# A two-layer pool and attention backbone: where the steps of the modulation chain are drawn

## The chip, the cores and the metric

The kernel runs on one core of one Trainium2 chip. The metric is device time in microseconds (us) of one execution, given as the median of several runs. One further execution was taken with the hardware profiler; all rows below are from it, and their times count from the start of its span.

## The reference, cut to what matters

Layer 0 is a pooling mixer, layer 1 a latent attention; both get their shift, scale and gate from a modulation: SiLU of a conditioning vector times a 2048 x 6144 matrix per layer.

```
for i in range(DEPTH):                       # 2 layers: pool, attention
    shift, scale, gate = split(silu(c) @ ada_w[i] + ada_b[i], 3)      # the same with c_ctx for the context
    h_lat = rms_norm(x, pre_norm[i]) * (1 + scale) + shift            # 512 latent tokens
    h_ctx = rms_norm(ctx, pre_norm[i]) * (1 + scale_c) + shift_c      # 256 context tokens
    ...
    x = x + gate * rms_norm(y_lat, post_norm[i])

def pool_branch(h, w_in, w_grp, b_grp, scale, w_out):                 # width 2048, 4 groups
    u, gate = split(h @ w_in, 2)
    p = centred_multiscale_pool(u)
    p = einsum('blgc,gcd->blgd', p, w_grp) + b_grp
    return (p * scale * silu(gate)) @ w_out
```

Only the pooling layer and the modulation bear on this change; the attention layer runs after it, untouched.

## The kernel before, in words

**Matrix products.** Every product is made of three passes (`mm3`, L198 to L200): each operand is split in a high and a low part, and high x high, high x low and low x high are summed in one PSUM bank. Weights come in pieces of 128 x 1024 values (`wpiece`, L178): a DMA on SyncE's queue (SP) fills one of two `raw` buffers (L186), ScalarE casts it to `whi` (L188), VectorE subtracts to `wlo` (L189); there are four `whi`/`wlo` pairs, and a `raw` buffer is free again when its `wlo` is made.

**The pooling layer** runs in this order. Eight pairs of columns (`gemm1`, j = 0 to 7) give u; eight more, the gate pairs (j = 8 to 15), give the gate: two 128-column blocks over 16 k-tiles, four weight pieces each, and `after(k4)` is called behind each piece. After a gate pair ScalarE copies a column (`gb`, L628) and makes SiLU (`sg`, L631) out of the two halves' banks, with a cast for a later weight piece queued between the halves, VectorE multiplies by the pooled part (L633), and a DMA stores `z1d`. Then `products` (L670) multiplies z by `pool_w_out` in four groups of 512 columns (cc = 0 to 3), eight pieces each; `ahead(n)` is called ahead of each piece of group n. The first group starts in banks that the last gate pair used. `load_z` (L432) brings z back from `z1d`, 128 rows at a time, on the SP queue, and ScalarE (L439) and VectorE (L440) split it into `aL` and `cbig`: four of these tiles are loaded during the last gate pair (into `s2` buffers), twelve during the first group (into three `xt` buffers).

**The modulation chain** (`chain`, `ada_part`, L446) has 128 steps. A step loads 128 x 1024 values of `ada_w` on the SP queue into one of two `araw` buffers (L454) and VectorE adds them, times one SiLU value per row, to two accumulators (L461 twice). After 16 steps TensorE transposes the accumulators (`sums`, L145, 16 transposes in four fours) and VectorE reduces them (L146); the next 16 steps need the accumulators back. `fill(n)` (L519) adds n to a due count and draws that many steps at its place in the program. Before, it is called with 1.4 behind each piece of pairs 1 to 7, 2.2 behind each piece of pairs 8 to 15, 0.4 ahead of each piece of group 0 and 0.9 ahead of those of groups 1 to 3.

**What sets the order.** Each engine and each queue runs its instructions in the order they were put on it. That order is made by a scheduler from the program: it follows the program's order, but takes an instruction early where it reckons the engine free. So a step drawn at one place can stand some way ahead of it on VectorE and on SP.

Of the kernel before, what the change touches and what calls it, by code (L numbers as in the profile page):

```python
# [80 lines left out]
def hybrid_kernel(  # L81
# [176 lines left out]
    def cxs(p, m):  # L258

        at = (4 + m) * 512  # L260
        return banks[:, at:at + CTX + 2]
# [170 lines left out]
    def load_z(z_of, k2):  # L432

        for kt in (2 * k2, 2 * k2 + 1):
            zr = z_of()[:, 0:KEYS]
            nc.sync.dma_start(out=zr, in_=z1d[kt])
            s = pools[:, kt:kt + 1]
            for dst, lo, n in ((aL[kt], 0, SEQ), (aC[:, kt], SEQ, CTX)):
                nc.scalar.activation(dst[:, 0, :], zr[:, lo:lo + n], AF.Copy, scale=s)  # L439
                nc.vector.scalar_tensor_tensor(dst[:, 1, :], zr[:, lo:lo + n], s, f32(dst[:, 0, :]),  # L440
                                               ALU.mult, ALU.subtract)
# [66 lines left out]
    with pool("pa") as ap:  # L508
# [16 lines left out]
        def fill(n):  # L525
            nonlocal due, taken
            due += n
            while due > 0.5:
                due -= 1
                taken += 1  # L530
                next(ada_steps, None)
# [5 lines left out]
        def u_in(ps):  # L537
            for m, u in enumerate(ub):
                nc.scalar.copy(u[:, 3 * PAD + SEQ:3 * PAD + KEYS], cxt(ps, m))
                nc.scalar.copy(u[:, PAD:PAD + SEQ], lat(ps, m))  # L540

        def u_out(g, m, pieces):


            u = ub[m]
            w = WINDOWS[g]
            h = w // 2
            s, step, n = u, 1, ULEN
            while step < w:
                n -= step  # L550
                s2 = ap.tile([P, ULEN], F32, name="s2", tag="s2", bufs=2)
                nc.vector.tensor_add(s2[:, :n], s[:, :n], s[:, step:step + n])
                s, step = s2, 2 * step
            b0 = PAD - h
            at = 0
            for lo, n in ((b0, h), (b0 + SEQ - h + 1, 2 * PAD + w - 1), (b0 + SPAN - h + 1, h - 1)):
                if n:
                    nc.vector.tensor_mul(s[:, lo:lo + n], s[:, lo:lo + n], edget[:, g, at:at + n])
                at += n
            nc.vector.scalar_tensor_tensor(s[:, b0:b0 + SPAN], s[:, b0:b0 + SPAN], 1.0 / w, u[:, PAD:PAD + SPAN],  # L560
                                           ALU.mult, ALU.subtract)
            hi = ap.tile([P, SPAN], F32R, name="ph", tag="ph", bufs=4)
            lo = ap.tile([P, SPAN], F32R, name="pl", tag="pl", bufs=4)
            nc.scalar.copy(hi, s[:, b0:b0 + SPAN])
            nc.vector.tensor_sub(lo, s[:, b0:b0 + SPAN], f32(hi))
            pieces.append((hi, lo))

        def gemm1(col, ways, after):

            ps = pair()  # L570
            for k4 in range(4):
                piece = wblock(w_in[k4 * 4 * P:(k4 + 1) * 4 * P, col:col + 2 * P], 4, 2 * P)
                todo = [(m, way, k) for k in range(4) for m in range(2) for way in ways]
                if k4 == 0:
                    todo.sort(key=lambda t: t[1] is ways[1])
                for m, (fn, a_), k in todo:
                    kt = 4 * k4 + k
                    mm3(fn(ps, m), wt(piece, k, m * P, P), a_(kt), kt == 0, kt == KT - 1)
                after(k4)
            return ps  # L580

        def group(g, pieces):

            for pr_ in range(2):
                wg = wblock(pool_w_grp[0, g, :, pr_ * 2 * P:(pr_ + 1) * 2 * P], 4, 2 * P)
                ps = pair()
                for fn, lo, n in ((lat, 0, SEQ), (cxt, SEQ + 2 * PAD, CTX)):
                    for m in range(2):
                        for k in range(4):
                            hi, low = pieces[k]  # L590
                            mm3(fn(ps, m), wt(wg, k, m * P, P), (hi[:, lo:lo + n], low[:, lo:lo + n]), k == 0, k == 3)
                for m in range(2):
                    dt = g * 4 + pr_ * 2 + m
                    yo = ap.tile([P, KEYS], F32, name="sg", tag="sg", bufs=3)
                    for fn, lo, n in ((cxt, SEQ, CTX), (lat, 0, SEQ)):
                        nc.scalar.activation(yo[:, lo:lo + n], fn(ps, m), AF.Identity, bias=poolb[:, dt:dt + 1])
                    nc.gpsimd.dma_start(out=y1d[dt], in_=yo)
# [3 lines left out]
        NP = 2 * GROUPS  # L601
        pieces = [[] for _ in range(GROUPS)]
        u_in(first)
        for j in range(1, 2 * NP):
            if j == NP:
                assert taken >= 32
            if j == 2 * NP - 1:
                assert taken >= 96
            def after(k4):
                if j <= NP and k4 < 2:  # L610
                    u_out((j - 1) // 2, k4, pieces[(j - 1) // 2])
                fill(1.4 if j < NP else 2.2)
                if j == 2 * NP - 1 and k4 in (1, 2):
                    load_z(lambda: ap.tile([P, ULEN], F32, name="s2", tag="s2", bufs=2), k4 - 1)

            ps = gemm1(j * 2 * P, WAYS if j < NP else GATES, after)
            if j < NP:
                u_in(ps)
            else:
                gated = []  # L620
                for m in range(2):
                    yin = ap.tile([P, ULEN], F32, name="s2", tag="s2", bufs=2)[:, 0:KEYS]
                    nc.gpsimd.dma_start(out=yin, in_=y1d[2 * (j - NP) + m])
                    sg = ap.tile([P, KEYS], F32, name="sg", tag="sg", bufs=3)
                    gated.append((sg, yin))
                gb = small.tile([P, 2, 2], F32, name="gb")
                for m in range(2):
                    nc.scalar.copy(gb[:, m], cxs(ps, m)[:, CTX:])  # L628
                for v, fn, lo, n in ((1, cxs, SEQ, CTX), (0, lat, 0, SEQ)):
                    for m in range(2):  # L630
                        nc.scalar.activation(gated[m][0][:, lo:lo + n], fn(ps, m)[:, 0:n], AF.Silu, bias=gb[:, m, v:v + 1])  # L631
                for m, (sg, yin) in enumerate(gated):
                    nc.vector.tensor_mul(sg, sg, yin)  # L633
                    nc.gpsimd.dma_start(out=z1d[2 * (j - NP) + m], in_=sg)
            if j % 2 == 0 and j <= NP:
                group(j // 2 - 1, pieces[j // 2 - 1])
# [26 lines left out]
    with pool("pb") as bp:  # L663
# [68 lines left out]

        def ahead(n):
            def step(k2):
                fill(0.4 if n == 0 else 0.9)
                if n in (0, 3):
                    (x_ahead if n else z_ahead)(k2)
            return step
# [465 lines left out]
```

## Time and profile before

| | |
|---|---|
| median of 3 runs | 1925.75 us (1922.88 to 1927.26) |
| profiled execution: its own time, its span | 1930.69 us, 1928.8 us |
| TensorE matmuls | 1875.1 us busy, 97% of the span |
| VectorE | 1190.4 us, 62% |
| ScalarE | 652.3 us, 34% |
| DMA, mean over the span | 155 GB/s |
| chain that ended last | TensorE 79%, DMA 10%, VectorE 6% |

TensorE is the engine to look at: it is busy nearly all the time, so a microsecond counts only where TensorE waits, or where its granted clock is low. Its busy time is a model (matmuls are pipelined), so distances between starts of matmuls are the surer measure. The rows read from the trace stand in a section of their own.

### The profile page before, as it was taken

To read this page: it belongs to the slowest core of one execution; us is meant where nothing else is said; L and a number is where in the kernel's file an instruction comes from. 1 tells how busy PE (TensorE), PEld (TensorE's weight loads), DVE (VectorE), ACT (ScalarE), POOL (GpSimd) and SP (SyncE) were. 2 spreads that over 40 slices of the span, in tenths; PEclk is the share of its full clock that TensorE was granted. 3 is DMA by queue.
4 is the path that set the end of the run, shared out by engine and by line. 5 is a ranking of instruction groups with operands and counts; after the bars stand their busy time and mean duration, and the time that the engine had idled before them with its cause. 6 is when DMAs were issued, how large, how long until landed. Compare 5 with 4: busy or idle time off the path is not lost.

```text
span 1928.8 us, 26041 instructions
## 1 busy us (share of the span) xinstructions
PE 1875.1 (97%) x10458; PEld 1618.6 (84%) x10458; DVE 1190.4 (62%) x1516; ACT 652.3 (34%) x1024; POOL 110.7 (6%) x201
## 2 busy tenths in 40 slices
PE   5999999999999979999999999999999999999998
PEld 3788888888888867887888988778999999998886
DVE  5778395877588878634764255635566667665333
ACT  6632222212111124223743232124434444444230
POOL 1000000000000000001010002200000000000000
PEclk9999999999999999999999999999999999999999
DMA  8746273557577777644751237843111112116334
GB/s 301 246 147 197 85 229 99 186 169 232 172 251 228 238 268 229 194 147 162 269 171 44 76 88 254 291 142 93 56 40 54 56 50 67 50 60 191 104 125 153
DMA packets 168105, 299.74 MB, mean 155 GB/s; under 512 B 19592, under 2 KB 89504, under 8 KB 166704
## 3 DMA queue, kind: packets, MB, share of 16 engines
q1 hardware_dynamic: 152800, 243.84, 39.6%
q0 software_dynamic: 13872, 52.07, 7.9%
q10 hardware_dynamic: 1312, 2.16, 0.3%
q8 instruction: 82, 1.34, 0.3%
q14 instruction: 39, 0.32, 0.1%
HBM read 268.65 MB, written 29.38 MB: 155 GB/s over the span
## 4 chain that ended last, share of the span: by engine, by line
PE 79%; DMA 10%; DVE 6%; issue 2%; ACT 2%; POOL 1%; SPq 0%; DVEq 0%; POOLq 0%; ACTq 0%
PE banks L198 24%; PE banks L199 24%; PE banks L200 24%; DMA garaw<-in_ada_w 3%; DMA araw<-in_ada_w 2%; PE banks L1087 2%; DVE acc L461 2%; DMA raw<-in_ada_w 1%; DVE wlo L189 1%; PE banks L1066 1%; PE banks L1067 1%; DMA xt<-z1d 1%; PE banks L145 1%; DMA xs<-in_x 1%; PE banks L227 1%
## 5 line engine op out<-in xcount | busy, mean ns | idle before, releaser
L189 DVE TENSOR_TENSOR wlo<-raw,whi 128x1024 fp32r<-128x1024 f32 (+1 forms) x276 | 328.8, 1195 | 316.0 <-ACT whi L188 314.5
L188 ACT CAST whi<-raw 128x1024 fp32r<-128x1024 f32 (+1 forms) x276 | 283.5, 1029 | 675.4 <-PE banks L200 245.9
L461 DVE SCALAR_TENSOR_TENSOR acc<-araw,sc,acc 128x1024 f32<-128x1024 f32 x240 | 297.6, 1280 | 45.1 <-DMA araw<-in_ada_w 44.7
L198 PE MATMUL banks<-aL,whi 128*128 128x512 f32 x768 | 303.8, 396 | 4.0 <-ACT sg L817 2.0
L200 PE MATMUL banks<-aL,wlo 128*128 128x512 f32 x768 | 302.4, 394 | 2.9 <-DVE wlo L189 2.9
L199 PE MATMUL banks<-aL,whi 128*128 128x512 f32 x768 | 303.3, 395 | 0.0
L199 PE MATMUL banks<-cbig,whi 128*128 128x256 f32 (+2 forms) x640 | 188.4, 294 | 0.0
L198 PE MATMUL banks<-cbig,whi 128*128 128x256 f32 (+2 forms) x640 | 187.8, 294 | 0.4 <-ACT cbig L290 0.4
L200 PE MATMUL banks<-cbig,wlo 128*128 128x256 f32 (+2 forms) x640 | 187.3, 293 | 0.0
L198 PE MATMUL banks<-whi,aL 128*128 128x512 f32 (+1 forms) x448 | 164.8, 368 | 10.4 <-ACT gb L628 6.9
L200 PEld LDWEIGHTS banks<-aL,wlo 128*128 128x128 f32 x768 | 144.7, 188 | 34.9 <-DVE wlo L189 4.2
L199 PE MATMUL banks<-wlo,aL 128*128 128x512 f32 (+1 forms) x448 | 164.2, 367 | 0.0
L200 PE MATMUL banks<-whi,aL 128*128 128x512 f32 (+1 forms) x448 | 164.0, 367 | 0.1
L198 PEld LDWEIGHTS banks<-aL,whi 128*128 128x128 f32 x768 | 145.0, 189 | 20.4 <-ACT aL L290 3.7
L199 PEld LDWEIGHTS banks<-aL,whi 128*128 128x128 f32 x768 | 145.4, 189 | 14.6
L198 PEld LDWEIGHTS banks<-cbig,whi 128*128 128x128 f32 x640 | 120.3, 188 | 21.6 <-ACT cbig L290 1.3
L199 PEld LDWEIGHTS banks<-cbig,whi 128*128 128x128 f32 x640 | 120.5, 188 | 19.7
L199 PE MATMUL banks<-wlo,cbig 128*128 128x256 f32 (+2 forms) x384 | 123.8, 322 | 1.9 <-DVE wlo L189 1.8
L198 PE MATMUL banks<-whi,cbig 128*128 128x256 f32 (+2 forms) x384 | 124.8, 325 | 0.1
L200 PEld LDWEIGHTS banks<-cbig,wlo 128*128 128x128 f32 x640 | 121.3, 189 | 3.4
L200 PE MATMUL banks<-whi,cbig 128*128 128x256 f32 (+2 forms) x384 | 123.5, 322 | 0.0
L198 PEld LDWEIGHTS banks<-whi,aL 128*128 128x128 f32 x448 | 84.8, 189 | 23.9 <-ACT gb L628 7.2
(234 smaller groups left out, 3294.3 us busy)
## 6 DMA issues: line engine op xcount, KB each, us to landing
araw<-in_ada_w SPq DMA_DIRECT2D x128, 512.0 KB, 4.3
raw<-in_pool_w_in SPq DMA_DIRECT2D x64, 512.0 KB, 4.8
raw<-in_pool_w_out SPq DMA_DIRECT2D x60, 512.0 KB, 4.7
raw<-in_mla_w_in SPq DMA_DIRECT2D x40, 512.0 KB, 4.0
raw<-in_ada_w SPq DMA_DIRECT2D x32, 512.0 KB, 4.8
garaw<-in_ada_w POOLq DMA_DIRECT2D x32, 512.0 KB, 5.5
raw<-in_mla_w_out SPq DMA_DIRECT2D x32, 512.0 KB, 3.9
raw<-in_mla_w_ukv SPq DMA_DIRECT2D x32, 256.0 KB, 3.3
```

What stands on the lines that cost most here:

```text
L145: nc.tensor.transpose(pt[:, k * P:(k + 1) * P], acc[:, (lo + k) * P:(lo + k + 1) * P], ident)
L188: nc.scalar.copy(hi[:, :n], raw[:, :n])
L189: nc.vector.tensor_sub(lo[:, :n], raw[:, :n], f32(hi[:, :n]))
L198: nc.tensor.matmul(o, l[0], r[0], start=start, stop=False)
L199: nc.tensor.matmul(o, l[0], r[1], start=False, stop=False)
L200: nc.tensor.matmul(o, l[1], r[0], start=False, stop=stop)
L227: nc.tensor.transpose(pt[:, t * P:(t + 1) * P], xt[:, kt * P:(kt + 1) * P], ident)
L461: nc.vector.scalar_tensor_tensor(acc[v], raw, w, acc[v], ALU.mult, ALU.add)
L1066: nc.tensor.matmul(to, qr[:, o], krh[:, ks], start=True, stop=False)
L1067: nc.tensor.matmul(to, qr[:, o], krl[:, ks], start=False, stop=False)
L1087: nc.tensor.transpose(pt[:, t * P:(t + 1) * P], pr[:, t * P:(t + 1) * P], ident)
```

## The change

`fill` is no longer called in the last gate pair (j = 15), nor ahead of the first four pieces of output group 0. Instead the other pairs draw a tenth more per piece (1.5 and 2.3), and from the fifth piece of group 0 on every piece draws 0.85.

```
             def after(k4):
                 if j <= NP and k4 < 2:
                     u_out((j - 1) // 2, k4, pieces[(j - 1) // 2])
-                fill(1.4 if j < NP else 2.2)
+                if j < 2 * NP - 1:
+                    fill(1.5 if j < NP else 2.3)
                 if j == 2 * NP - 1 and k4 in (1, 2):
                     load_z(lambda: ap.tile([P, ULEN], F32, name="s2", tag="s2", bufs=2), k4 - 1)
...
         def ahead(n):
             def step(k2):
-                fill(0.4 if n == 0 else 0.9)
+                fill(0.85 if n or k2 >= 4 else 0)
                 if n in (0, 3):
                     (x_ahead if n else z_ahead)(k2)
             return step
```

In the program's order the count drawn at the end of pair 14, of pair 15 and of group 0 was 101, 110 and 113; it is now 106, 106 and 110. The lines behind the change move down by one (L628 is now L629, L633 is L634, L683 is L684).

The SP queue around the last gate pair, before, from the second piece of `pool_w_out` on (`araw` is a step's load, `s_...` a z tile for the first group):

```order
L186 DMA raw<-in_pool_w_out 128x2x512
L436 DMA s_5552<-z1d 128x768
L454 DMA araw<-in_ada_w 128x1024 x2
L436 DMA s_5620<-z1d 128x768
L454 DMA araw<-in_ada_w 128x1024
L436 DMA s_5626<-z1d 128x768
L454 DMA araw<-in_ada_w 128x1024 x4
L186 DMA raw<-in_pool_w_out 128x2x512
L454 DMA araw<-in_ada_w 128x1024
L186 DMA raw<-in_pool_w_out 128x2x512
L454 DMA araw<-in_ada_w 128x1024
L186 DMA raw<-in_pool_w_out 128x2x512
```

Seven step loads stand there between the second and the third piece of `pool_w_out`.

The same place of the SP queue, changed:

```order
L186 DMA raw<-in_pool_w_out 128x2x512
L436 DMA s_5556<-z1d 128x768
L454 DMA araw<-in_ada_w 128x1024
L436 DMA s_5616<-z1d 128x768
L454 DMA araw<-in_ada_w 128x1024
L436 DMA s_5622<-z1d 128x768
L186 DMA raw<-in_pool_w_out 128x2x512
L454 DMA araw<-in_ada_w 128x1024 x2
L186 DMA raw<-in_pool_w_out 128x2x512
L454 DMA araw<-in_ada_w 128x1024
L186 DMA raw<-in_pool_w_out 128x2x512 x2
L436 DMA xt<-z1d 128x768 x3
```

Two of the seven are left there; steps 108 to 114 still load in this stretch, hoisted from group 0 and group 1.

VectorE at the same place, before, from the second z tile on (`acc` is half a step; the L189 row is the first piece of `pool_w_out`):

```order
L440 SCALAR_TENSOR_TENSOR aL_92<-s_5552,vc_113,aL_92 128x512
L461 SCALAR_TENSOR_TENSOR acc<-araw,sc,acc 128x1024 x2
L440 SCALAR_TENSOR_TENSOR cbig<-s_5552,vc_113,cbig 128x256
L461 SCALAR_TENSOR_TENSOR acc<-araw,sc,acc 128x1024 x2
L440 SCALAR_TENSOR_TENSOR aL_93<-s_5620,vc_113,aL_93 128x512
L461 SCALAR_TENSOR_TENSOR acc<-araw,sc,acc 128x1024 x2
L440 SCALAR_TENSOR_TENSOR cbig<-s_5620,vc_113,cbig 128x256
L440 SCALAR_TENSOR_TENSOR aL_94<-s_5626,vc_113,aL_94 128x512
L440 SCALAR_TENSOR_TENSOR cbig<-s_5626,vc_113,cbig 128x256
L461 SCALAR_TENSOR_TENSOR acc<-araw,sc,acc 128x1024 x4
L189 TENSOR_TENSOR wlo<-raw,whi 128x1024
L461 SCALAR_TENSOR_TENSOR acc<-araw,sc,acc 128x1024 x2
```

The first `wlo` of `pool_w_out` stands behind all four z tiles and, counted from the gate product of pair 14, behind 14 half steps.

VectorE at the same place, changed:

```order
L440 SCALAR_TENSOR_TENSOR aL_92<-s_5556,vc_113,aL_92 128x512
L440 SCALAR_TENSOR_TENSOR cbig<-s_5556,vc_113,cbig 128x256
L189 TENSOR_TENSOR wlo<-raw,whi 128x1024
L461 SCALAR_TENSOR_TENSOR acc<-araw,sc,acc 128x1024
L440 SCALAR_TENSOR_TENSOR aL_93<-s_5616,vc_113,aL_93 128x512
L440 SCALAR_TENSOR_TENSOR cbig<-s_5616,vc_113,cbig 128x256
L461 SCALAR_TENSOR_TENSOR acc<-araw,sc,acc 128x1024
L440 SCALAR_TENSOR_TENSOR aL_94<-s_5622,vc_113,aL_94 128x512
L440 SCALAR_TENSOR_TENSOR cbig<-s_5622,vc_113,cbig 128x256
L461 SCALAR_TENSOR_TENSOR acc<-araw,sc,acc 128x1024 x2
L189 TENSOR_TENSOR wlo<-raw,whi 128x1024
L461 SCALAR_TENSOR_TENSOR acc<-araw,sc,acc 128x1024 x2
```

The first `wlo` has moved up to behind the second z tile and four half steps.

## Rows read from the trace of the kernel before

**Rows 1.** TensorE's waits, 690 to 905 us: in total, times, longest.
```profile
PE banks L198 <- ACT gb L628: 6.9, 1, 6.9
PE banks L198 <- ACT aL L439: 2.6, 1, 2.6
PE banks L145 <- DVE pc L146: 1.0, 1, 1.0
PE banks L198 <- ACT sg L631: 0.9, 1, 0.9
```
**Rows 2.** Busy time by stretch: from:to, length, PE, PEld, DVE, ACT, POOL, clock, DMA.
```profile
663.00:697.70 34.70, 34.70 (x199) 30.46 (x199) 30.09 (x31) 9.55 (x17) 2.19 (x4) 1.00 0.76 255
...
705.40:710.00 4.60, 3.69 (x8) 2.48 (x8) 4.60 (x5) 2.04 (x4) 0.00 (x0) 0.62 0.86 261
710.00:718.90 8.90, 8.86 (x38) 7.05 (x38) 3.34 (x4) 1.05 (x1) 1.64 (x3) 1.00 0.96 320
718.90:726.20 7.30, 4.64 (x13) 3.33 (x13) 4.50 (x7) 4.77 (x9) 0.00 (x0) 0.77 0.76 274
...
759.70:803.20 43.50, 43.50 (x193) 36.04 (x192) 38.55 (x36) 11.07 (x17) 0.55 (x1) 1.00 0.69 221
```
**Rows 3.** TensorE in order of time: start, length, what, idle before it and its releaser.
```profile
645.25 1.04 PE L145 MATMUL banks<-ident,acc 128*128 128x128 f32 x8
...
697.73 0.39 PE L198 MATMUL banks<-whi,aL 128*128 128x512 f32 x1
698.04 0.50 PE L199 MATMUL banks<-wlo,aL 128*128 128x512 f32 x1
705.45 0.79 PE L198 MATMUL banks<-whi,aL 128*128 128x512 f32 x1 [6.91 <-ACT gb L628]
...
718.57 0.39 PE L200 MATMUL banks<-whi,aL 128*128 128x512 f32 x1
721.55 0.50 PE L198 MATMUL banks<-whi,aL 128*128 128x512 f32 x1 [2.60 <-ACT aL L439]
```
**Rows 4.** ScalarE in order of time, at the ends of pairs 14 and 15.
```profile
663.14 0.16 ACT L628 COPY gb<-banks 128x2 f32<-128x2 f32 x1 [6.46 <-PE banks L200]
...
665.26 1.08 ACT L631 ACTIVATE sg<-banks,gb 128x256 f32<-128x256 f32 x2
...
703.20 1.04 ACT L188 CAST whi<-raw 128x1024 fp32r<-128x1024 f32 x1 [13.10 <-DMA raw<-in_pool_w_out]
...
707.99 1.05 ACT L188 CAST whi<-raw 128x1024 fp32r<-128x1024 f32 x1 [2.54 <-DMA raw<-in_pool_w_out]
...
720.78 0.72 ACT L439 ACTIVATE aL<-xt,vc 128x512 fp32r<-128x512 f32 x1 [6.18 <-DMA xt<-z1d]
```
**Rows 5.** SyncE's queue in order of time: the DMAs it issues.
```profile
686.91 10.29 SPq L454 DMA_DIRECT2D araw<-in_ada_w  x4
698.06 0.38 SPq L186 DMA_DIRECT2D raw<-in_pool_w_out  x1
...
712.49 0.38 SPq L186 DMA_DIRECT2D raw<-in_pool_w_out  x1
712.98 2.18 SPq L436 DMA_DIRECT2D xt<-z1d  x3
```
**Rows 6.** VectorE in order of time, from the end of step 80 on.
```profile
585.00 1.29 DVE L146 TENSOR_REDUCE pc<-banks 128x4 f32<-128x512 f32 x2 [2.03 <-PE banks L145]
...
639.80 4.87 DVE L461 SCALAR_TENSOR_TENSOR acc<-araw,sc,acc 128x1024 f32<-128x1024 f32 x4
...
668.81 0.95 DVE L633 TENSOR_TENSOR sg<-sg,s 128x768 f32<-128x768 f32 x1
...
696.77 1.22 DVE L189 TENSOR_TENSOR wlo<-raw,whi 128x1024 fp32r<-128x1024 f32 x1
...
710.89 1.22 DVE L189 TENSOR_TENSOR wlo<-raw,whi 128x1024 fp32r<-128x1024 f32 x1
```
**Rows 7.** The page's DMA issues: count, size, median us from issue to landing.
```profile
raw<-in_pool_w_out SPq DMA_DIRECT2D x60, 512.0 KB, 4.7
```

More of the change, by code (lines that the diff above doesn't have):

```diff
@@ L611, in after @@
                     u_out((j - 1) // 2, k4, pieces[(j - 1) // 2])
-                fill(1.4 if j < NP else 2.2)
+                if j < 2 * NP - 1:
+                    fill(1.5 if j < NP else 2.3)
                 if j == 2 * NP - 1 and k4 in (1, 2):
@@ L734, in step @@
             def step(k2):
-                fill(0.4 if n == 0 else 0.9)
+                fill(0.85 if n or k2 >= 4 else 0)
                 if n in (0, 3):
```

## The prediction, made before the changed kernel ran

> **What bounds the kernel now.** TensorE does: it is busy 97% of the span, so I look only for places where it waits or runs slow. Read in this order: TensorE's waits give, for the 215 us from the gate pairs' end to the end of `products`, four lines that sum to 11.4 us [rows 1]. The stretches then show where: in the last gate pair TensorE is busy 34.70 of 34.70 us at clock 1.00, while in two stretches of the first output group its clock is 0.62 and 0.77, so part of each runs at the lower of its two levels, 1.2 GHz instead of 2.4 [rows 2]. The next group is the yardstick: 193 matmuls in 43.50 us, 0.226 us each, no wait [rows 2]. TensorE's own rows say what each stop costs by distances between starts [rows 3]: the first two matmuls of the group go at 697.73 and 698.04, the third at 705.45, so 7.41 - 0.23 = 7.2 us are lost; from 718.57 to 721.55 2.98 - 0.23 = 2.75 us. A stop of 0.9 us for the second SiLU and one of 1.0 us at the transposes come on top [rows 1]. The slow clock: 8 matmuls in 3.69 us cost 3.69 - 8 x 0.226 = 1.9 us, 13 in 4.64 us cost 1.7 us [rows 2]. Sum of what stands here to be had: 7.2 + 2.75 + 0.9 + 1.0 + 1.9 + 1.7 = **15.4 us**.
>
> Why the 7.2 us: the third matmul needs a bank that ScalarE's SiLU of pair 15 reads. ScalarE runs in order, and in front of that SiLU stands the cast of the third piece of `pool_w_out`, which came at 703.20 after 13.10 us of waiting for its load [rows 4]. That load was issued at 698.06, after four step loads had held the SP queue from 686.91 to 697.20 [rows 5]. It could not have gone earlier anyway: its buffer is the first piece's, whose `wlo` ran from 696.77 to 697.99, behind the half steps on VectorE [rows 6]. So both queues held it up, and both by steps of the chain. The later stop has the same root: the `xt` load of 712.98 stands on SP behind a weight load at 712.49 [rows 5], which had waited for a `wlo` of 710.89 to 712.11 [rows 6]; the tile reached ScalarE at 720.78 [rows 4].
>
> **The change part by part.** *Out of the last pair.* In the order, the first `wlo` stood 14 half steps behind the gate product of pair 14; now four stand there, and the third and fourth z tile have moved behind it too. The half steps cost 4.87 / 4 = 1.22 us [rows 6]: 10 x 1.22 = 12.2 us of VectorE gone from 696.77 - 668.81 = 28.0 us, which leaves 15.8 us, a little less for the two z tiles. The gate product itself may come later, since about half a step more stands ahead of it per 16 (the transposes of the 96th step stand 92 matmuls earlier, some 17 us, and 107 steps instead of 102 stand before it; 16 steps took 644.67 - 585.00 = 59.7 us, 3.7 us each [rows 6], so five more are 18.5 us): 671 instead of 668.81. Then `wlo` ends at 671 + 15.8 + 1.2 = 688 at the latest, more likely 686. The third piece's load goes then, with no step in front of it that still waits, and needs 5.1 us as it did (698.06 to 703.20) [rows 4, 5]: it is cast by 692 to 694. Pair 15's first half is ready for SiLU near 697. The cover is thus 3 to 5 us, and the 7.2 us and their 1.9 us of slow clock go, but for 0.2. If that cover is gone, each microsecond beyond costs one.
>
> *What is late next: the fourth piece.* The end of a gate pair takes ScalarE from its first copy at 663.14 to 666.34 [rows 4], with a weight cast between the halves. Here it is the fourth piece's, whose load waits for the second `wlo` (four half steps, 4.9 us, and two z tiles further on: 693 to 695) and takes 4.7 us [rows 7]: 698 to 700. The cast cannot start ahead of 698 either, since its buffer is freed by pair 15's last piece. So the second half's SiLU ends between 700.2 and 702, and TensorE, with ten matmuls to do first, asks at 700. I take 1.0 us, bounds 0 and 3.
>
> *The z tiles of the first group.* The fourth `wlo` now ends near 701, so the sixth weight load and behind it the `xt` load issue near 701.6 instead of 712.98. The load took 720.78 - 712.98 = 7.8 us while DMA ran at 0.96 of its time and 320 GB/s [rows 2]; the median of a bigger load is 4.7 us [rows 7]. So it lands between 706.3 and 709.4, and the split is done 0.7 us later [rows 4]. TensorE asks after 48 matmuls, at 697.73 + 10.9 + 1.2 = 709.8. I take 0.5 us left of 2.75, bounds 0 and 3, and no slow clock: the 0.9 us wait was followed by a stretch at 1.00 [rows 2]. The Trainium skill (DMA: Bandwidth & Descriptors, Anatomy of one DMA) gives a fixed 2.0 us plus the bytes at 436 GB/s, fitted for the gpsimd path: an estimate by it is 2.9 us for this tile. By the page nothing at all would be left to wait for here, 0.5 us less than I sum; the row's 7.8 us speaks against it, and the row decides.
>
> *Moved steps.* No step goes away. A tenth more per piece means 0.4 steps more per pair, 0.4 x 3.7 = 1.5 us of VectorE's and SP's time in a pair; VectorE was idle 4.6 us even in pair 15 [rows 2], and TensorE has four pieces of weights ahead. I cost it at nothing; uncovered it is the slow rival below. Behind the middle of group 0 the rest of the chain runs through groups 1 and 2, with as many steps between two `wlo` as group 1 had before while TensorE did not wait [rows 2]. The 16 transposes of step 112 move from group 0 to group 1, those of step 128 later into group 3; their own time moves along, and of their 1.0 us wait I keep 0.5, bounds 0 and 2.
>
> Left: 0.2 + 1.0 + 0.5 + 0.5 = 2.2 of 15.4 us, a gain of 13.2. The profiled execution took 1930.7 us, so 1917.5 by this profile; the median lies 4.9 us below that execution, and with the same gain it becomes **1912.5**. Bounds of this case from the three left-over waits: 2.2 may be 0 or 8, so a gain of 15.4 to 7.4, 1910 to 1918, with the spread of the runs 1908 at the low end.
>
> **The rivals.** *Half a gain.* Fourth piece and `xt` tile both come at their late bounds, 3 us each, and the clock falls again, 1.7 us: 2.2 + 2 + 2.5 + 1.7 = 8.4 us left, a gain of 7, or 5 if both are later still: 1918 to 1921. For it: SP still carries three step loads between the weight loads, and each load's landing varied from 4.7 to 7.8 us.
>
> *It does not do what it says.* The order shows steps 108 to 114 in the last pair all the same, hoisted by the scheduler. If the z tiles land late there (each `wlo` stands behind one), the first `wlo` ends after 692 and SiLU stays locked behind the third cast: at 697 the wait is the old one, 1923 to 1928. Against it: 12.2 us of VectorE work is gone from that stretch in any case.
>
> *Slower.* The chain becomes TensorE's bound in the gate pairs. 16 steps took 59.7 us, and TensorE's transposes for step 96 came at 645.25, 0.6 us after the last half step ended at 644.67 [rows 3, 6]; at step 80 VectorE had waited 2.0 us for TensorE, so there was room [rows 6]. The changed order keeps about the same distance, 340 matmuls or 61 us, between the transposes. From 61 us per 16 steps on, every microsecond more is a wait of TensorE at step 80 and again at step 96, and the gate product of pair 14 comes that much later, which takes back the first gain. At 66 us: 5 + 5 us, slow clock twice, 3.6, the old stop kept: +10 to +14 us, 1936 to 1940. For it: hardly any slack in the row; against it: VectorE has two gate products less to do between steps 80 and 96 in the new order, 1.9 us.
>
> **How the numbers follow.** Forecast 0.70; half a gain 0.15; not what it says 0.09; slower 0.06. The range, 1908 to 1921, holds the forecast and half a gain nearly whole, about 0.81. A measurement of this kernel tells about 0.2% from no change, 3.9 us, so faster is below 1921.9: 0.70 + 0.15 and none of the rest, set at 0.84 for the tails; same 0.09; slower 0.07.
>
> **What the changed profile would show.** TensorE's third matmul of group 0 within 1 us of the second; no cast of ScalarE ahead of pair 15's first copy that waits for `pool_w_out`; the third weight load issued near 687, the first `xt` load near 702; clock 1.00 through group 0. The forecast is wrong if a wait of several us stands at that third matmul (steps still in the way), ahead of the fifth k-tile of group 0 (`xt`), or at TensorE's transposes in pairs 12 to 14 (chain too slow).

## The result, and the profile after

The changed kernel takes **1913.1 us** (median of 4 runs, 1911.1 to 1916.7) against 1924.3 us (1922.8 to 1927.3) of the kernel before, run beside it: ratio 0.9942, 95% interval 0.9922 to 0.9962, a gain of 11.2 us (7.3 to 15.0). Forecast were 1912.5 us and a gain of 13.2. The profiled execution of the changed kernel took 1912.9 us with a span of 1911.1, where that of before took 1930.7; the difference of these two, 17.8 us, is larger than that of the medians, because the profiled execution of before was longer than its timed runs.

TensorE's waits of the changed kernel, 690 to 905 us, answer to [rows 1] (in total, times, longest):

```profile
PE banks L199 <- DVE wlo L189: 2.0, 1, 2.0
```

All four waits of before are gone. The one row that is left stands near 894 us, behind the products. But the stretch 100 to 690 us, where before had no wait of TensorE, now has one row:

```profile
PE banks L145 <- DVE pc L146: 2.5, 2, 1.4
```

These are the transposes of steps 80 and 96 (569.34 and 632.18 us). So there is a new wait in the gate pairs.

Busy time by stretch, which answers to [rows 2] (from:to, length, PE, PEld, DVE, ACT, POOL, clock, DMA share, GB/s); pair 15, then four stretches of the first output group, then the next group:

```profile
665.00:699.80 34.80, 34.80 (x200) 30.56 (x199) 27.54 (x28) 11.61 (x21) 2.18 (x4) 1.00 0.80 268
699.80:707.50 7.70, 7.70 (x34) 6.00 (x34) 3.94 (x4) 3.22 (x6) 1.63 (x3) 1.00 0.84 242
707.50:712.00 4.50, 4.50 (x22) 3.72 (x21) 1.48 (x3) 1.46 (x3) 0.00 (x0) 1.00 1.02 411
712.00:721.00 9.00, 9.00 (x42) 7.44 (x41) 6.87 (x10) 6.58 (x12) 0.00 (x0) 1.00 0.82 277
721.00:742.30 21.30, 21.30 (x96) 17.64 (x95) 12.66 (x19) 11.58 (x20) 0.00 (x0) 1.00 0.60 190
748.50:792.00 43.50, 43.50 (x201) 35.87 (x200) 32.92 (x32) 11.07 (x16) 0.00 (x0) 1.00 0.59 189
```

TensorE is busy in every microsecond of the first group, at a granted clock of 1.00; the two stretches of 0.62 and 0.77 of before went with the stops. The price of the whole is read from two starts on each side, the first matmul of the products and VectorE's last product with the gate (`y`). Before it is 697.73 [rows 3] and this row:

```profile
891.95 2.13 DVE L683 TENSOR_TENSOR y<-banks,gp 128x512 f32<-128x512 f32 x3
```

After it is these two, from TensorE's and VectorE's rows in order of time:

```profile
699.63 0.39 PE L198 MATMUL banks<-whi,aL 128*128 128x512 f32 x1
700.10 0.47 PE L198 MATMUL banks<-whi,aL 128*128 128x512 f32 x1
...
877.59 2.13 DVE L684 TENSOR_TENSOR y<-banks,gp 128x512 f32<-128x512 f32 x3
```

That is 194.2 us before and 178.0 after: **16.3 us** less in the products. The first matmul of the products comes 1.9 us later than before (699.63 against 697.73), so their end comes 14.4 us earlier (877.59 against 891.95). The other 3.3 us by which the spans differ lie behind the products, where nothing was changed; that part took between 1031.8 and 1038.0 us in the traces of this case. The third matmul, at 700.10, now follows the first two without a stop, where [rows 3] had 7.4 us between them.

How the order of events changed is read from the queues. ScalarE in order of time (start, length, what, idle before it and its releaser), which answers to [rows 4]:

```profile
683.76 1.04 ACT L188 CAST whi<-raw 128x1024 fp32r<-128x1024 f32 x1
...
688.51 1.04 ACT L188 CAST whi<-raw 128x1024 fp32r<-128x1024 f32 x1
691.25 1.06 ACT L188 CAST whi<-raw 128x1024 fp32r<-128x1024 f32 x1 [1.70 <-PE banks L199]
698.77 0.16 ACT L629 COPY gb<-banks 128x2 f32<-128x2 f32 x1 [6.46 <-PE banks L200]
...
705.52 1.05 ACT L188 CAST whi<-raw 128x1024 fp32r<-128x1024 f32 x1 [3.56 <-PE banks L200]
709.13 0.72 ACT L439 ACTIVATE aL<-xt,vc 128x512 fp32r<-128x512 f32 x1 [2.55 <-DMA xt<-z1d]
```

The third piece's cast, at 691.25, is 7.5 us ahead of pair 15's first copy at 698.77, and no cast ahead of that copy waits for a load of `pool_w_out` any more. The SP queue, which answers to [rows 5]:

```profile
686.08 0.38 SPq L186 DMA_DIRECT2D raw<-in_pool_w_out  x1
689.54 3.78 SPq L454 DMA_DIRECT2D araw<-in_ada_w  x2
694.13 0.38 SPq L186 DMA_DIRECT2D raw<-in_pool_w_out  x1
...
697.65 5.02 SPq L186 DMA_DIRECT2D raw<-in_pool_w_out  x2
703.09 1.47 SPq L436 DMA_DIRECT2D xt<-z1d  x3
```

VectorE, which answers to [rows 6]: gate product of pair 14, then the first, second and fourth `wlo` of `pool_w_out`.

```profile
669.78 0.95 DVE L634 TENSOR_TENSOR sg<-sg,s 128x768 f32<-128x768 f32 x1
...
684.83 1.22 DVE L189 TENSOR_TENSOR wlo<-raw,whi 128x1024 fp32r<-128x1024 f32 x1 [0.19 <-ACT whi L188]
692.87 1.23 DVE L189 TENSOR_TENSOR wlo<-raw,whi 128x1024 fp32r<-128x1024 f32 x1
...
701.05 1.23 DVE L189 TENSOR_TENSOR wlo<-raw,whi 128x1024 fp32r<-128x1024 f32 x1
```

### The profile page after: what moved, and what is told of

Read it like the earlier page. It is cut to its first block, busy times and chain, and to the rows that moved or that the text cites. A ratio compares the mean times of both kernels' runs of the same rounds, so it can differ in the third digit from the quotient of the medians.

```text
span 1911.1 us, 26041 instructions
## 1 busy us (share of the span) xinstructions
PE 1869.0 (98%) x10458; PEld 1617.9 (85%) x10458; DVE 1192.3 (62%) x1516; ACT 652.8 (34%) x1024; POOL 110.3 (6%) x201
## 4 chain that ended last, share of the span: by engine, by line
PE 82%; DMA 8%; DVE 5%; issue 3%; ACT 1%; POOL 0%; SPq 0%; DVEq 0%; POOLq 0%; ACTq 0%
PE banks L198 25%; PE banks L199 25%; PE banks L200 25%; DMA araw<-in_ada_w 3%; DMA garaw<-in_ada_w 2%; PE banks L1088 2%; DVE acc L461 2%; DVE wlo L189 1%; PE banks L1067 1%; PE banks L1068 1%; DMA raw<-in_ada_w 1%; PE banks L145 1%; DMA xs<-in_x 1%; PE banks L227 1%; ACT whi L188 0%
## 5 line engine op out<-in xcount | busy, mean ns | idle before, releaser
L189 DVE TENSOR_TENSOR wlo<-raw,whi 128x1024 fp32r<-128x1024 f32 (+1 forms) x276 | 328.5, 1195 | 275.7 <-ACT whi L188 274.0
L200 PEld LDWEIGHTS banks<-aL,wlo 128*128 128x128 f32 x768 | 144.3, 188 | 32.6 <-DVE wlo L189 1.8
L199 PEld LDWEIGHTS banks<-aL,whi 128*128 128x128 f32 x768 | 144.8, 189 | 14.4
L1074 ACT ACTIVATE pr<-banks,nm 128x768 f32<-128x768 f32 x64 | 57.7, 902 | 134.0 <-DVE nm L1071 133.9
```

The source lines that it names most:

```text
L189: nc.vector.tensor_sub(lo[:, :n], raw[:, :n], f32(hi[:, :n]))
L199: nc.tensor.matmul(o, l[0], r[1], start=False, stop=False)
L200: nc.tensor.matmul(o, l[1], r[0], start=False, stop=stop)
L1074: nc.scalar.activation(pr, ps[:, 0:KEYS], AF.Exp, bias=nm, accum_out=zs)
```

## The experiments

Three questions: which part of the change carries the gain, whether VectorE or the SP queue is what held ScalarE and the z tiles, and where the new 2.5 us come from. The kernel before was run beside each group of experiments: 1925.0, 1924.4 and 1924.4 us.

**Only the last pair emptied.** The changed kernel with a draw in all of group 0:

```diff
-                fill(0.85 if n or k2 >= 4 else 0)
+                fill(0.85 if n else 0.4)
```

> The changed kernel, with 0.4 steps drawn ahead of every piece of output group 0 again: only the last gate pair is emptied. If the half steps and step loads ahead of the first wlo of pool_w_out carry the gain (pair 15), nothing is lost: third matmul of group 0 within 1 us of the second, 1912 to 1916 us against 1924 of before and 1913 of the change. If the gain comes from the first half of group 0 being empty, the z tiles stall again: 2 to 4 us of waits there, and the time is 1917 to 1922.

Measured: 1912.9 us (ratio 0.9935, 0.9922 to 0.9948), no wait of TensorE in group 0. The empty first half of group 0 brings nothing. In the order, nothing changes ahead of step 112 between this kernel and the changed one: the steps of group 0's first half had been hoisted out of it anyway.

**Only group 0 emptied.** Before, with `fill(0.85 if n or k2 >= 4 else 0)` as its only edit:

> Before, with the draws of output group 0 alone changed (none ahead of its first four pieces, 0.85 from the fifth on); the pairs draw 1.4 and 2.2 as before, pair 15 too. If pair 15 carries the gain, the stop of about 7 us at the third matmul of group 0 and the slow clock behind it stay, and with them most of the time: 1920 to 1925 us. If group 0 carries it, 1913 to 1916 us and no stop.

Measured: 1924.7 us (1.0001, 0.9992 to 1.0011). The two largest of TensorE's waits from 690 to 905 us [rows 1] stand there again, the two small ones do not:

```profile
PE banks L198 <- ACT gb L628: 6.8, 1, 6.8
PE banks L198 <- ACT aL L439: 3.0, 1, 3.0
```

In this trace the end of the products (`y` at 889.14 us) comes 11.6 us later than in the changed kernel (877.59); the medians differ by as much. So the gain comes from the pairs. But the pairs were edited twice, and the next run takes these edits apart.

**Emptied, at the old rates.** The changed kernel with

```diff
-                    fill(1.5 if j < NP else 2.3)
+                    fill(1.4 if j < NP else 2.2)
...
-                fill(0.85 if n or k2 >= 4 else 0)
+                fill(0.98 if n or k2 >= 4 else 0)
```

> Last pair and first half of group 0 empty as in the change, but the other pairs draw 1.4 and 2.2 as before, and the later pieces 0.98 instead of 0.85. If the raised rate made the new 2.5 us of TensorE's waits at its transposes (steps 80 and 96), they go to below 0.5 us, and the time is 1910 to 1912 us, 1 to 3 below the change, less what a later z tile of group 0 may cost (up to 2 us). If something else made them, 2 to 3 us stay at the transposes and the time is that of the change, 1913 to 1915.

Measured: 1923.9 us (0.9996, 0.9986 to 1.0006). Both expectations missed. The wait at the transposes is gone, as one of them said, but so is the whole gain. TensorE, 690 to 905 us:

```profile
PE banks L198 <- ACT aL L439: 10.1, 1, 10.1
PE banks L199 <- DVE wlo L189: 1.9, 1, 1.9
```

The stop at the third matmul is gone (pair 15 is empty), but one of 10.1 us stands now at the first z tile of group 0, with a clock of 0.55 in the stretch 711 to 722 us. The SP queue of this kernel shows why:

```profile
697.23 0.38 SPq L186 DMA_DIRECT2D raw<-in_pool_w_out  x1
698.43 8.60 SPq L454 DMA_DIRECT2D araw<-in_ada_w  x3
708.73 0.38 SPq L186 DMA_DIRECT2D raw<-in_pool_w_out  x1
709.23 1.61 SPq L436 DMA_DIRECT2D xt<-z1d  x3
```

Three step loads stand in front of the weight load and the `xt` loads; in the changed kernel none stands there. The weight load at 708.73 could not have gone earlier, though, since its buffer is freed by this `wlo`, which ends at 708.67:

```profile
707.45 1.22 DVE L189 TENSOR_TENSOR wlo<-raw,whi 128x1024 fp32r<-128x1024 f32 x1
```

Counting VectorE's half steps in the order up to the first `xt` tile gives a plain rule: before, after, and both kernels above have **224 half steps, 112 steps, there**, this one too. Wherever the steps are drawn, the scheduler pulls them forward until step 112, behind which the accumulators have to be transposed. So an empty pair 15 does not take the steps away from ahead of the z tiles. What takes them away is drawing more of the 112 earlier: 106 by the end of pair 14 in the changed kernel, 101 before and here. The raised rate, which I had costed as a mere price, is a part of the gain.

The next four runs test this. (The expectations below say 110 and 103 drawn steps for two of them; by the rounding of `fill` it is 111 and 104.)

**The same count at the old rate of the gate pairs**, `fill(1.6 if j < NP else 2.2)`:

> The changed kernel with 1.6 steps per piece in pairs 1 to 7 and 2.2 in the gate pairs: as in the change, 106 steps are drawn by the end of pair 14, but at the old rate in the gate pairs. New theory, after the run with the old rates: the scheduler hoists step loads from behind until step 112, where the accumulators must first be transposed, so what counts is how many of the 112 are still to be drawn at the end of pair 14 (here 6, and 7 step loads stand ahead of the first xt load, as in the change): no stop in group 0, 1910 to 1914 us. Rival, that the higher rate of the gate pairs itself is needed: a stop at the z tiles and 1920 to 1924 us.

Measured: 1912.6 us (0.9934, 0.9922 to 0.9947), no wait in group 0 and none at the transposes. It is the count that matters, not the rate of the gate pairs.

**Nearly all of the 112 ahead**, `fill(1.75 if j < NP else 2.2)`:

> The changed kernel with 1.75 steps per piece in pairs 1 to 7 and 2.2 in the gate pairs: 110 steps are drawn by the end of pair 14, so two are left until step 112, and two step loads stand ahead of the first xt load instead of seven. By the theory of the steps left until 112: no stop in group 0, and the first xt load goes 3 to 6 us earlier than in the change; nothing waits there any more, so 1909 to 1913 us, the same as the change. If steps are hoisted past 112, or pairs 1 to 7 can't take 7 steps each: waits of several us at the transposes there or at the z tiles, 1916 to 1925 us.

Measured: 1919.6 us (0.9974, 0.9962 to 0.9985). Group 0 has no stop at the z tiles, as expected, but the `xt` load is not earlier: it goes 4.3 us after pair 15's first copy, exactly as in the changed kernel (703.09 - 698.77), though two step loads stand ahead of it instead of seven. The floor is the pair's own end: the fourth cast stands on ScalarE behind the copies of pair 15, then come the fourth `wlo`, the sixth weight load and the `xt` load. And there are new waits of TensorE from 400 to 550 us, of which the changed kernel has none:

```profile
PE banks L198 <- ACT sg L596: 2.5, 1, 2.5
PE banks L200 <- DVE wlo L189: 1.7, 2, 1.3
PE banks L145 <- DVE pc L146: 0.5, 1, 0.5
```

They do not stand in pairs 1 to 7, which took their seven steps each without a wait: pair 7's result was copied at 402 us, and the waits stand at 433 to 466 us, in the first gate pairs, and at the transposes of step 80, at 548 us. That steps pushed back from pairs 1 to 7 make them is likely, not shown. With 1.9 us at the transposes of step 112, which now fall into group 0, TensorE waits 6.6 us here, against the changed kernel's 2.5 us at the transposes of steps 80 and 96: 4.1 us more. The profiled executions differ by 4.0 us (1916.9 and 1912.9), the medians by 6.5; what is left of these is not placed.

**A count between**, `fill(1.5 if j < NP else 2.2)` and 0.92 behind:

> Pair 15 and the first half of group 0 empty, 1.5 steps per piece in pairs 1 to 7, 2.2 in the gate pairs, 0.92 behind: 103 steps are drawn by the end of pair 14, 9 are left until step 112, and 10 step loads stand ahead of the first xt load (7 in the change, 11 with the old rates). By the theory of the steps left: a stop at the z tiles of group 0 of about 10.1 - 2.9 = 7 us, 1918 to 1922 us. If the count doesn't matter, no stop and 1911 to 1914 us, or the whole 10 us and 1924.

Measured: 1921.8 us (0.9986, 0.9977 to 0.9995). The stop at the z tile, expected at 7 us:

```profile
PE banks L198 <- ACT aL L439: 6.3, 1, 6.3
```

Another 1.6 us stand at the transposes of step 96. The traces of this run and of the next are of executions 4.4 and 4.0 us below their medians.

**The rates alone**, before with `fill(1.5 if j < NP else 2.3)` in all pairs, pair 15 too:

> Before, with the rates of the pairs alone raised (1.5 and 2.3, in pair 15 too; 0.4 in group 0): step 112 falls into pair 15, and 12 step loads stand ahead of the first xt load, as in before. By the theory of the steps ahead, a stop of 7 to 12 us stays at the third matmul of group 0 or at its z tiles: 1921 to 1930 us. If the raised rate alone makes the gain: 1912 to 1916 us.

Measured: 1923.8 us (0.9996, 0.9987 to 1.0005). TensorE, 690 to 905 us:

```profile
PE banks L145 <- DVE pc L146: 4.2, 1, 4.2
PE banks L198 <- ACT aL L439: 3.6, 1, 3.6
```

The third matmul does not wait here, but the transposes of step 112 and the z tile do: pair 15's own draws have carried the chain past 112, and 119 step loads stand ahead of the first `xt` load. Neither half of the edit of the pairs brings anything by itself; both together bring 11 us.

**A higher rate**, the changed kernel with 2.5 in the gate pairs:

> The changed kernel with 2.5 steps per piece in the gate pairs instead of 2.3. If 16 steps of the chain take VectorE about 60 us whatever the rate, the transposes, now 290 matmuls (some 52 us) apart, each wait 6 to 8 us for it: three to four times, 20 to 30 us in all, 1933 to 1943 us. If VectorE had idle time left in the pairs to take the steps in, the waits stay below 5 us in all, and the time is 1912 to 1917.

Measured: 1939.9 us (1.0082, 1.0067 to 1.0098). TensorE's waits, 100 to 690 and 690 to 905 us:

```profile
PE banks L145 <- DVE acc L461: 12.0, 2, 7.1
...
PE banks L198 <- ACT aL L439: 8.8, 1, 8.8
```

The time is as expected of a chain that keeps to about 60 us per 16 steps, but its make-up is not: two waits of 7.1 and 4.9 us at transposes instead of three or four, and 8.8 us at the z tile. Nor is it VectorE's work alone that sets this pace: from the transposes of step 80 to those of step 96 (557.28 to 617.11 us) VectorE was busy 49.9 of 59.8 us and waited 9.5 us for step loads. The chain has two `araw` buffers; whether a third would shorten it was not tried. At this rate exactly 112 steps are drawn by the end of pair 14, the barrier falls into the pair, and the scheduler hoists the next steps: 124 loads stand ahead of the first `xt` load.

The kernels with an empty pair 15 make a row (counted in the order; the distance from pair 15's first copy to the first `xt` load, and the stop, from the traces):

| steps drawn by the end of pair 14 | step loads from the first piece of `pool_w_out` to the first `xt` load | first `xt` load after pair 15's first copy | stop at its tile |
|---|---|---|---|
| 111 | 2 | 4.3 us | 0 |
| 106 (changed kernel; group 0 drawn; 1.6 and 2.2) | 7 | 4.3 us | 0 |
| 104 | 10 | 10.4 us | 6.3 us |
| 101 (old rates) | 11 | 13.5 us | 10.1 us |
| 112 (2.5) | 12 | 13.7 us | 8.8 us |

**VectorE or the SP queue?** First, before with the loads of steps 102 to 111, but without their additions:

```diff
-                for v in range(2):
+                for v in range(0 if 101 < taken < 112 else 2):
```

> Before, with the loads of steps 102 to 111 kept on the SP queue and their VectorE additions left out (their share of the modulation is missing). No half step stands ahead of the first wlo any more, seven step loads still stand on SP between the first and the second piece of pool_w_out. If VectorE's half steps hold the first wlo and with it ScalarE's SiLU, the stop of about 7 us at the third matmul is gone: 1911 to 1916 us. If the loads on the SP queue do it, third piece and SiLU stay late: a stop of 4 us or more, 1918 to 1925 us.

Measured: 1917.9 us (0.9963, 0.9950 to 0.9977). With every load still on SP the stop at the third matmul is gone; what is left in group 0 ahead of its transposes is 2.0 us at the z tile:

```profile
PE banks L198 <- ACT aL L439: 2.0, 1, 2.0
```

The time lies 2 us above what I expected; transposes in group 0 wait for another 1.9 us. But the loads are not where they were: seven of them now stand between the first and the second piece of `pool_w_out` (659.75 and 678.59), and only two between the second and the third (684.69). And a load without additions has no half step to wait for. So this run shows that the additions matter, and not yet that the queue does not; the next one takes the queue away and keeps the additions.

Second, before with these loads on GpSimd's queue and the additions in place:

```diff
-                nc.sync.dma_start(out=raw, in_=ada_w[...])
+                (nc.gpsimd if 101 < taken < 112 else nc.sync).dma_start(out=raw, in_=ada_w[...])
```

> Before, with the loads of steps 102 to 111 issued by GpSimd, off the SP queue; VectorE's work is whole, and 12 half steps stand ahead of the first wlo (14 in before). If VectorE holds the first wlo, it ends near 694 instead of 698, and a stop of 2 to 6 us stays at the third matmul: 1917 to 1923 us. If the SP queue does it: no stop, 1911 to 1916 us.

Measured: 1929.3 us (1.0035, 1.0021 to 1.0048). SP has no step load between the first and the third piece here, and yet the third piece goes no earlier than its buffer is freed. VectorE's first `wlo`, SP's next weight load, and ScalarE's cast of it:

```profile
694.39 1.22 DVE L189 TENSOR_TENSOR wlo<-raw,whi 128x1024 fp32r<-128x1024 f32 x1
```
```profile
695.67 3.87 SPq L186 DMA_DIRECT2D raw<-in_pool_w_out  x2
```
```profile
700.88 1.04 ACT L188 CAST whi<-raw 128x1024 fp32r<-128x1024 f32 x1 [11.68 <-DMA raw<-in_pool_w_out]
```

The load goes 0.06 us behind the end of that `wlo` (695.61), as it did before with the step loads in the queue (698.06 behind 697.99 [rows 5, 6]). The third matmul stops for 5.4 us. So **VectorE's half steps** are what holds ScalarE's SiLU, not the loads in the queue. The time itself came out 6 us above the expected range; where these lie I could not read from its one trace, whose products take about as long as before's, so that stays open.

Third, the same move of the loads in the kernel with the old rates and an empty pair 15, whose z tile stopped TensorE for 10.1 us:

> The run with the old rates and an empty pair 15 (a stop of 10.1 us at the z tiles of group 0, 1923.9 us), with the loads of steps 102 to 111 issued by GpSimd, off the SP queue; VectorE has the same half steps. If the step loads on the SP queue ahead of the first xt load make that stop, it shrinks below 2 us: 1911 to 1915 us. If the half steps on VectorE make it, through the wlo that free the raw buffers: 5 to 10 us stay, 1918 to 1924 us.

Measured: 1931.1 us (1.0043, 1.0030 to 1.0055). Both expectations missed: the stop neither went nor stayed, it grew. TensorE's wait, and the SP queue:

```profile
PE banks L198 <- ACT aL L439: 16.3, 1, 16.3
```
```profile
683.28 19.43 SPq L186 DMA_DIRECT2D raw<-in_pool_w_out  x3
705.93 0.34 SPq L454 DMA_DIRECT2D araw<-in_ada_w  x1
711.97 0.37 SPq L186 DMA_DIRECT2D raw<-in_pool_w_out  x1
714.03 0.34 SPq L454 DMA_DIRECT2D araw<-in_ada_w  x1
714.47 1.80 SPq L436 DMA_DIRECT2D xt<-z1d  x3
```

Two step loads are left on SP, and the `xt` load is 5 us later, not earlier. Three weight loads take 19.43 us, because each waits for a `wlo` behind half steps on VectorE; and the step load at 714.03 still puts the `xt` load 2 us behind the weight load of 711.97. So the stop does not need the ten step loads on SP. But this run does not show that the half steps alone make it. From the second gate product of pair 14 to the third `wlo` VectorE has 13 half steps in both kernels, and yet takes 32.6 us here against 28.3: it waited 5.6 us for z tiles on ScalarE, against 2.2, and 3.7 us for step loads, against 2.5. How late the loads land counts too.

**The changed kernel once more**, unaltered:

> The changed kernel itself, unaltered, beside the others. 1911 to 1915 us. If the 2.5 us that TensorE waited at the transposes of steps 80 and 96 in its first profile belong to the program, 1.5 to 3.5 us stand there again; if they were that one execution's, below 0.5 us, as in the run that emptied pair 15 alone, whose program is the same up to there.

Measured: 1912.8 us (0.9946, 0.9933 to 0.9960), and at the transposes of steps 80 and 96:

```profile
PE banks L145 <- DVE pc L146: 2.4, 2, 1.2
```

The wait came back, so it was not an accident of one execution. Yet the trace with only the last pair emptied, whose instructions are the same in kind and order up to step 112, shows none. Its half steps between the transposes of steps 64 and 80 waited 9.0 us for their loads, those of the changed kernel 10.4 and 9.9 us in its two traces; between those of steps 80 and 96 it was 9.6 us against 11.6 and 11.6. So the margin at these transposes is one to two microseconds of load time; why the loads come later in one of two kernels with the same order stays open. The medians do not show the wait: 1912.9 us without it, 1913.1 and 1912.8 with it. No version beat the changed kernel: 1912.6 to 1913.1 us for the four runs with 106 steps drawn early is one time.

## Why the prediction was right, point by point

**What was to be had.** 15.4 us by stops and slow clock, 16.3 us by the length of the products. Right for this pair of traces; but the profiled execution of before was a long one. The trace with only group 0 emptied, which has before's time, has products of 191.9 us, 13.9 more than the changed kernel.

**Out of the last pair.** Gate product of pair 14 at 671, measured 669.78; first `wlo` done by 686, measured 684.83 + 1.22 = 686.05; third load 687, measured 686.08; its cast by 692 to 694, measured 692.3, held for its last 1.7 us by a `whi` buffer that TensorE still read, not by the load. The cover was 6.5 us and not 3 to 5. The run with the loads on GpSimd's queue confirms the cause that the sum rests on, half steps on VectorE; my sentence that both queues held it up was half wrong: at this place the step loads on SP cost no more than 0.07 us.

**The fourth piece.** Second half's SiLU by 700.2 to 702, measured 701.96. TensorE did not wait for it; of the 1.0 us that I kept, nothing was needed.

**The z tiles.** `xt` load at 701.6, measured 703.09, with products that start 1.9 us later; tile on ScalarE by 709.4, measured 709.13. Waits: none, against 0.5 kept. From issue to first use the load took 703.09 to 709.13, 6.0 us, while all queues together moved 279 GB/s. The Trainium skill (DMA: Bandwidth & Descriptors, Anatomy of one DMA), whose fit is for the gpsimd path, would give an estimate of 2.9 us; the trace does not agree, for a load on SP's queue with others under way. The reason that I gave for the early `xt` load was incomplete: I named the earlier fourth `wlo`, and that holds at 106 drawn steps; with an equally empty pair and 101 steps, eleven step loads and a stop of 10.1 us stand there. I had counted the half steps ahead of the first `wlo`, and not those ahead of the sixth weight load.

**Moved steps.** Here the prediction failed in size: "I cost it at nothing" became 2.5 us at the transposes of steps 80 and 96 in the traces, the place that the slow rival had named. That the kernel at a higher rate took 1939.9 us, inside that rival's 1936 to 1940, is luck: the rival had 16 steps take 66 us and the old stop kept, and in that run they took about 60, with 8.8 us at the z tile. The 2.2 us kept as left over did not come either, so two terms of about the same size and opposite sign were wrong. That the forecast of 13.2 us lies between the 14.4 us by which the products end earlier in the two traces and the 11.2 of the medians is in part luck too; 11.2 is the measure, and 13.2 lies within its interval.

**The rivals.** Half a gain, by a late z tile: not in this kernel, but two draws fewer by the end of pair 14 bring it, with 1921.8 us. That the change does not do what it says: half true. All 112 steps still stand ahead of the first `xt` tile; only their distance from it has changed.

## What to carry to other kernels

When work is moved in the source of a kernel whose order a scheduler makes, look for what stops the scheduler (here the transposes that free the accumulators), and count the work between that barrier and the critical stretch; a place left empty in the source is filled from behind. A filler's rate is then chosen so that most of a section is done ahead of the stretch, without its barrier falling into the stretch. And where a DMA queue seems to hold a load up, ask first whose buffer the load waits for: here two weight loads behind step loads went 0.06 to 0.07 us after the buffer's last reader on VectorE, and the stops of 7 and 10 us went with the half steps ahead of that reader and the time that their own loads took.

## What the runs showed of the hardware

Step loads moved from the SP queue to GpSimd's made both kernels slower, by 5 us (1929.3 against 1924.4) and 7 us (1931.1 against 1923.9), though VectorE's additions stayed; in the second, the z tile's stop grew from 10.1 to 16.3 us. I had expected a gain or no change. The longest stops had the lowest granted clock: in the stretch of 5 to 11 us around the stop it was 1.00 with a stop of 2.0 us (706 to 711 us of the run without additions), 0.72 with 6.3 us (708 to 716 us), and 0.55 with 10.1 us (711 to 722 us). Below 1.00 part of the stretch ran at 1.2 instead of 2.4 GHz. The length of a stop alone does not settle it, though: around the stop of 2.6 us of before the clock was 0.77 [rows 2], around the one of 3.6 us of the rates alone 1.00 (715 to 725 us). A stop of 6.9 us stood 16 us ahead of the first, one of 4.2 us 25 us ahead of the second; why the clocks differ stays open.
